# First gate/up pair by plain block products, first down operands prepared earlier, and attention paced at 0.48

## The chip, the cores and the metric

The kernel runs on one core of one Trainium2 chip. The metric is device time in microseconds (us), from the launch of the program to its end; three runs of the kernel before gave 1980.32, 1982.52 and 1985.81 us, and the median, 1982.52 us, is the number to compare with. A profiled execution of its own is used for all reading of time inside the kernel.

The engines are named as the profile names them: PE does matmuls (PEld is its weight load), DVE and ACT do elementwise work, POOL does some elementwise work and issues DMAs, SP issues DMAs only. Each engine works through its own instruction list in order.

## The reference

Two batches go through one encoder layer with shared weights: the "prompt" (512 tokens) and the "sample" (1024 tokens), 1024 wide.

```python
h = rmsnorm(x, norm_mix_w)
proj = h @ w_in                       # 1024 x 4096: HGRN2 inputs and attention q, k, v
o_hgrn = gated linear recurrence, both directions, 4 heads
o_na = neighbourhood_attention(rmsnorm(q), rmsnorm(k), v, na_rpb)   # 8 heads, 16 x 64 grid
x = x + concat([o_hgrn, o_na]) @ w_out
h2 = rmsnorm(x, norm_ffn_w)
x = x + (silu(h2 @ w_gate) * (h2 @ w_up)) @ w_down      # 1024 x 2816, twice, and 2816 x 1024
```

All of it is float32. The kernel does each large product as three matmuls: an operand is split into a rounded high part and a low part, and high x high, high x low and low x high are added in PSUM.

## The kernel before, in words

The order of the work is written out as a list of units (an input projection group, one head of the recurrence, one gate/up column block, and so on), which `drive` runs one after the other, loading the weights of the next two ahead. Beside the units runs a second stream of work: `queue` and `active` hold generators (norms, recurrence halves, the attention of a batch), and `quantum()`, which every dense unit calls after 6 matmuls, adds `mix["rate"]` to a credit; each whole credit lets `micro()` take one step of one generator. So the rate is "steps of attention per 6 dense matmuls". A scheduler then places each engine's instructions from this order, so neighbours may be exchanged.

The places that the change touches:

- **The sample's attention** (`na_jobs("s")`) runs beside the prompt's output projection and its 22 gate/up units (`gate_units_p`, `mm_tr`, L180 to L182), at a rate of 0.43. A tile step of it has the value products L604, the transposes of the probabilities L618 and the logits L636. Before the fourth-last of those units `late()` runs: `finish()` issues whatever is left of the attention, its pool is closed, and `load_oT` loads the eight head outputs of both halves of the sample (`ost<-ot_s`, L927, POOL's queue) through two staging buffers, and splits each on ACT (L928) and DVE (L929) into the tiles `os`.
- **The sample's output projection** (`out_units`, `mm_nat`, L167 to L169) multiplies `os` by `w_out`. Four PSUM banks take four token tiles; the banks come free when DVE adds the input x (L950), which SP has loaded (L937) behind the weights in its queue.
- **The sample's gate/up** (`gate_s`). The 1024 x 1024 normed input is cut in four blocks (A11, A12, A21, A22: two halves of the tokens by two halves of the width), and each pair j of 128-column gate/up blocks is made by a Strassen-Winograd scheme: seven products P1 to P7 of 12 matmuls for the gate (w = 0) and seven for up (w = 1), instead of eight plain ones each. It needs the sums S1 to S4 of input blocks and T2, T3 and two more of weight blocks. In the first pair (j = 0) the input blocks are still being made: `run()` writes out by hand when a block is filled (`fill`: ACT cast L1040, DVE remainder L1041), when the sums are formed in place (L1161 to L1170, L1207), when weight operands are made (`ahead`) and when a product begins. The first pair's weight sums run on DVE, all later ones on POOL (L1101, L1109). `taken` turns the sums of products into silu(gate) * up. From j = 1 on a plain loop does all.
- **Buffers.** Weight operands sit in the ring `w` of 5 tiles of two slots; the raw input blocks in the pool `araw`, whose memory the pool `ev1` (the results of `taken`) takes over once it is closed; the split input blocks in `x1_s`, `actR1`, `actR2` (two tiles) and `aop`.
- **The down projection** (`down_all`) is Strassen-Winograd again, 7 x 11 steps of 18 matmuls; step n needs a split gate block `ao` (from the ring `w`) and a split weight block `bo` (its own pool, opened after the gate's pools are closed). Two steps are prepared ahead.

Of the kernel before, what the change touches and what calls it, by code (L numbers as in the profile page):

```python
# [46 lines left out]
def trunk(ctx, tc, x_p, x_s, nmw, w_in, lbw, gnw, qnw, knw, rpb, w_out, nfw, w_g, w_u, w_d,  # L47
# [1001 lines left out]
    def gate_s():  # L1049
# [38 lines left out]
        def weights(wsrc, j, eng):  # L1088


            r = []
            for g in range(2):
                t = (main if g else pls["tp"]).tile([128, 1024], F32, tag="wst", bufs=2, name="wst")
                ld.dma_start(out=t.rearrange("p (k c) -> p k c", k=4),
                             in_=wsrc[g * 512:g * 512 + 512, j * 256:j * 256 + 256]
                             .rearrange("(k p) c -> p k c", p=128))
                r.append(t.rearrange("p (k n c) -> p n k c", k=4, n=2))
            B = {"11": r[0][:, 0], "12": r[0][:, 1], "21": r[1][:, 0], "22": r[1][:, 1]}

            def sub(o, x, y):  # L1100
                eng.tensor_tensor(out=o, in0=x, in1=y, op=ALU.subtract)  # L1101

            def give(n):
                if n not in ("P1", "P2", "P3") and "T2" not in B:
                    t = pls["tp"].tile([128, 2, 512], F32, tag="t", bufs=1, name="t")
                    B["T2"], B["T3"] = (t[:, i, :].rearrange("p (k c) -> p k c", k=4)
                                        for i in range(2))
                    sub(B["T3"], B["22"], B["12"])
                    eng.tensor_tensor(out=B["T2"], in0=B["T3"], in1=B["11"], op=ALU.add)  # L1109
# [13 lines left out]
        order = [(0, w, n) for n in ("P1", "P2", "P4", "P5", "P6", "P7", "P3") for w in range(2)]  # L1123
        order += [(j, w, n) for j in range(1, NP) for w in range(2)
# [3 lines left out]
        def ahead(n):  # L1128
            while len(ready) < n and todo:
                j, w, p = todo.pop(0)  # L1130
                if (j, w) not in made:
                    made[j, w] = weights((w_g, w_u)[w], j, pool if j else dve)
                ready.append(made[j, w](p))
# [6 lines left out]
        ps = {}  # L1140

        def begin(n, w, f):

            ps[n, w] = f()
            product(ps[n, w], n, ready.pop(0), False)

        def start():
            place("A11", "x1_s")
            fill("A11", raw[0, 0])
            ahead(2)  # L1150
            place("A12", "actR1")
            fill("A12", raw[0, 1])
            ahead(4)
# [19 lines left out]
        def run():  # L1173
# [3 lines left out]
            begin("P1", 0, dense_ps)  # L1177
            need(("2", "s", 6))
            fill("A22", a22, first, 2)
            begin("P1", 1, dense_ps)  # L1180
            sums(first, 2)
            begin("P2", 0, dense_ps)
# [3 lines left out]
            begin("P2", 1, dense_ps)  # L1186
            fill("A22", a22, rest, 4)
            ahead(4)
            for w in range(2):
                begin("P4", w, mix_ps)  # L1190
            sums(rest, 4)
            place("S1", "actR2")
            fill("S1", a22)
            ahead(4)
            for w in range(2):
                begin("P5", w, mix_ps)
# [3 lines left out]
            fill("S2", a11)  # L1200
            ahead(4)
# [34 lines left out]

            for w in range(2):
                s[1, w] = tmp("s1", 2)
                act.copy(out=s[1, w], in_=ps["P1", w])
                taken(w, "A11", ps["P2", w], s[1, w])  # L1240
            for w in range(2):
                begin("P6", w, dense_ps)
                s[2, w] = plus(tmp("u2", 2), ps["P6", w], s[1, w])
            ahead(4)
            for w in range(2):
                product(ps["P6", w], "P7", ready.pop(0), True)
                s[3, w] = plus(s[1, w], ps["P6", w], s[1, w])
            ahead(7)
            for w in range(2):
                taken(w, "A22", ps["P5", w], s[3, w])  # L1250
                taken(w, "A21", ps["P4", w], s[3, w])
                product(ps["P5", w], "P3", ready.pop(0), True)
                taken(w, "A12", ps["P5", w], s[2, w])
            store_g(0, 0, 512, G, ev)
            bank = {"P1": "X", "P2": "X", "P4": "W", "P6": "Y", "P7": "Y", "P5": "Z", "P3": "Z"}
            for j, w, n in order[14:]:
                ahead(7)
                x = bank[n], w
# [22 lines left out]

    def down_all():
# [16 lines left out]
        def load(n):  # L1299
            if n >= len(steps):  # L1300
                return
            i, j = steps[n]
            a = (pl if n % 2 else main).tile([128, 1024], F32, tag="wst", bufs=2,
                                             name="wst")[:, :768]
            ld.dma_start(out=a, in_=g_d[order[i][0]][j])
# [72 lines left out]
        for n in range(2):  # L1378
            prep(n)
# [28 lines left out]
    def weave(a, b_):  # L1408
        r = []
        for x, y in zip(a, b_):  # L1410
# [21 lines left out]
                    set_mix(0.43, 1))  # L1432
# [71 lines left out]
```

## Time and profile before

| | us |
|---|---|
| median of three runs | 1982.52 |
| lowest, highest run | 1980.32, 1985.81 |
| profiled execution | 1981.45 |
| span of the profiled execution (first to last instruction) | 1979.7 |
| PE busy | 1930.4 |
| DVE, ACT, POOL busy | 1259.8, 825.7, 410.3 |

The profiled execution took 1981.45 us, of which the span is 1979.7 us and 1.75 us lie around it. PE is the engine to watch: it is busy for nearly the whole span. A row of the waits says which instruction of an engine waited for which other engine's. A row of the timeline is a run of equal instructions with the start of the first, the time to the end of the last, their count, and in brackets the idle time of the engine before them with what ended it. Matmuls are pipelined, so two rows of matmuls overlap by a little; their pace is read from start to start.

### The profile page before, as it was taken

The page shows a single profiled execution, that of the slowest core. Times are in us where ns is not written, and L with a number is a line of the kernel's source. Part 1 is how long each engine was busy: PE and PEld are TensorE (multiplying, and loading weights), DVE is VectorE, ACT ScalarE, POOL GpSimd, SP SyncE. Part 2 cuts the span into 40 slices and gives each one's busy share as a digit, 9 for nine tenths or more (in the row PEclk, how much of TensorE's full clock was granted, in tenths as well). Part 3 has the DMA queues.
Part 4 walks back from the last instruction along what each step waited for, and adds up shares of the span by engine and source line. Part 5 has one row for each costly group of instructions (what it writes and reads, how often), then busy time and mean ns, then how long its engine had stood idle before and what let it go on. Part 6 is the DMA issues. An engine that isn't in the chain of part 4 may idle for free.

```text
span 1979.7 us, 31155 instructions
## 1 busy us (share of the span) xinstructions
PE 1930.4 (98%) x11890; PEld 1551.9 (78%) x11890; DVE 1259.8 (64%) x2487; ACT 825.7 (42%) x1546; POOL 410.3 (21%) x416
## 2 busy tenths in 40 slices
PE   7999999999999999999999898999999999999999
PEld 5777787778788788888887676788888887888887
DVE  7687535575765667857555349766666665675643
ACT  5555445553543545645554226322322222333331
POOL 1200000000000010212213200646445533441400
PEclk9999999999999999999999999999999999999999
DMA  7832364432122164654444621233323327663442
GB/s 238 270 100 92 113 214 125 142 106 86 44 76 91 60 222 137 194 159 151 151 126 151 242 80 44 95 112 111 96 92 104 114 78 254 198 205 122 138 155 98
DMA packets 226508, 266.61 MB, mean 135 GB/s; under 512 B 19653, under 2 KB 161115, under 8 KB 226103
## 3 DMA queue, kind: packets, MB, share of 16 engines
q1 hardware_dynamic: 188448, 186.30, 30.6%
q0 software_dynamic: 12672, 38.80, 5.5%
q10 hardware_dynamic: 25239, 39.52, 5.5%
q8 instruction: 94, 1.54, 0.3%
q14 instruction: 55, 0.45, 0.1%
HBM read 194.72 MB, written 70.20 MB: 134 GB/s over the span
## 4 chain that ended last, share of the span: by engine, by line
PE 84%; DVE 7%; DMA 5%; issue 2%; ACT 2%; POOL 0%; ACTq 0%; SPq 0%; DVEq 0%; POOLq 0%
PE pd L1046 21%; PE pm L1046 16%; PE pd L180 7%; PE pd L167 6%; PE pd L181 6%; PE pd L182 6%; PE pd L168 6%; PE pd L169 6%; PE pm L312 2%; PE pm L604 2%; PE pm L618 1%; PE pm L636 1%; DMA ost<-ot_s 1%; PE pm L451 1%; DVE w L110 1%
## 5 line engine op out<-in xcount | busy, mean ns | idle before, releaser
L110 DVE TENSOR_TENSOR w<-wst,w 128x1024 fp32r<-128x1024 f32 x128 | 160.2, 1254 | 106.5 <-ACT w L109 105.7
L1046 PE MATMUL pd<-bo,ao 128*128 128x512 f32 x792 | 199.2, 398 | 3.4 <-DVE bo L1041 3.4
L109 ACT CAST w<-wst 128x1024 fp32r<-128x1024 f32 x128 | 134.3, 1050 | 143.5 <-PE pd L182 57.9
L1046 PEld LDWEIGHTS pd<-bo,ao 128*128 128x128 f32 x792 | 149.8, 189 | 40.0 <-DVE bo L1041 3.8
L1046 PE MATMUL pm<-bo,ao 128*128 128x512 f32 x594 | 151.0, 396 | 0.0
L180 PE MATMUL pd<-h2p,w 128*128 128x512 f32 (+1 forms) x368 | 142.0, 386 | 0.1
L181 PE MATMUL pd<-h2p,w 128*128 128x512 f32 (+1 forms) x368 | 141.0, 383 | 0.0
L182 PE MATMUL pd<-h2p,w 128*128 128x512 f32 (+1 forms) x368 | 140.9, 383 | 0.0
L927 POOL DMA_DIRECT2D ost<-ot_p x8 | 4.3, 540 | 624.8 <-ACT Kn L378 610.4
L1046 PEld LDWEIGHTS pm<-bo,ao 128*128 128x128 f32 x594 | 111.7, 188 | 27.0
L1046 PE MATMUL pm<-opS,w 128*128 128x512 f32 x528 | 129.2, 394 | 2.0 <-DVE sg L1219 1.5
L167 PE MATMUL pd<-w,hs 128*128 128x512 f32 x320 | 130.7, 408 | 0.0
L1046 PE MATMUL pd<-opS,w 128*128 128x512 f32 x528 | 129.2, 394 | 1.2 <-DVE u L1219 1.2
L1046 PE MATMUL pd<-opA,w 128*128 128x512 f32 x528 | 128.9, 393 | 0.0
L169 PE MATMUL pd<-w,hs 128*128 128x512 f32 x320 | 125.6, 393 | 0.0
L168 PE MATMUL pd<-w,hs 128*128 128x512 f32 x320 | 125.5, 392 | 0.0
L1046 PEld LDWEIGHTS pm<-opS,w 128*128 128x128 f32 x528 | 99.0, 188 | 25.6 <-DVE sg L1219 1.9
L1046 PEld LDWEIGHTS pd<-opS,w 128*128 128x128 f32 x528 | 99.0, 188 | 24.8 <-DVE u L1219 2.0
L1046 PEld LDWEIGHTS pd<-opA,w 128*128 128x128 f32 x528 | 99.0, 188 | 22.1
L1040 ACT CAST w<-wst 128x512 fp32r<-128x512 f32 x110 | 64.9, 618 | 122.5 <-PE pd L1046 59.3
L1041 DVE TENSOR_TENSOR w<-wst,w 128x512 fp32r<-128x512 f32 x110 | 102.5, 949 | 15.8 <-ACT w L1040 15.4
L1041 DVE TENSOR_TENSOR bo<-B,bo 128x512 fp32r<-128x512 f32 x55 | 53.5, 974 | 85.0 <-ACT bo L1040 85.0
(245 smaller groups left out, 4308.3 us busy)
## 6 DMA issues: line engine op xcount, KB each, us to landing
wst<-in_w_in_dram SPq DMA_DIRECT2D x68, 512.0 KB, 4.0
wst<-in_w_gate_dram SPq DMA_DIRECT2D x44, 512.0 KB, 3.8
wst<-in_w_up_dram SPq DMA_DIRECT2D x44, 512.0 KB, 3.8
wst<-g_S SPq DMA_DIRECT2D x44, 384.0 KB, 3.1
wst<-g_A SPq DMA_DIRECT2D x33, 384.0 KB, 3.6
g_S<-S POOLq DMA_DIRECT2D x44, 256.0 KB, 2.7
pj_s<-ev ACTq DMA_DIRECT2D x40, 256.0 KB, 2.2
bias<-bias_d SPq DMA_DIRECT2D x192, 48.0 KB, 2.8
```

Of the source, the lines that this page charges most:

```text
L109: act.copy(out=w[:, 0, :], in_=s)
L110: dve.tensor_tensor(out=w[:, 1, :], in0=s, in1=f32(w[:, 0, :]), op=ALU.subtract)
L167: pe.matmul(ps, lhsT=xh, rhs=w[:, 0, j, :], start=k == 0, stop=False)
L168: pe.matmul(ps, lhsT=xh, rhs=w[:, 1, j, :], start=False, stop=False)
L169: pe.matmul(ps, lhsT=xl, rhs=w[:, 0, j, :], start=False, stop=k == NK - 1)
L180: pe.matmul(ps[:, ts], lhsT=wv[:, 0, k, :], rhs=xh, start=k == 0, stop=False)
L181: pe.matmul(ps[:, ts], lhsT=wv[:, 0, k, :], rhs=xl, start=False, stop=False)
L182: pe.matmul(ps[:, ts], lhsT=wv[:, 1, k, :], rhs=xh, start=False, stop=k == NK - 1)
L312: pe.matmul(ps[i:i + n, c * n:c * n + n], lhsT=lhsT[:, c * 128 + i:c * 128 + i + n], rhs=rhs(c * 128 + i), start=True, stop=True)
L1040: act.copy(out=dst[0], in_=src)
L1041: dve.tensor_tensor(out=dst[1], in0=src, in1=f32(dst[0]), op=ALU.subtract)
L1046: pe.matmul(ps, lhsT=l[a], rhs=r[b_], start=start and i == 0, stop=stop and i == 2, skip_group_check=more)
```

## The change

Three things are changed.

1. The first pair of the sample's gate/up is made by plain products: for each of gate and up the output blocks 11, 12, 21 and 22 are two input blocks times two weight blocks each (24 matmuls, eight such groups). There is no weight sum and no sum of products for this pair; A21 is split as an operand of its own; S1 moves to the pool `aop`, S4 to `actR2`, in the tile that A21 had; the eight weight blocks of the first pair take eight slots of the ring, and three operands of the second pair are made before S4 is filled.
2. `down_first` loads and splits the operands of the down projection's first two steps. It is called ahead of the second-last product of the last pair, and takes its memory from the staging buffers and the ring of the gate's weights. The loop of `down_all` begins with these.
3. The rate of the sample's attention is 0.48 steps a quantum instead of 0.43.

```diff
-        def weights(wsrc, j, eng):
+        def weights(wsrc, j):
...
             def give(n):
+                if n in B:
+                    o = slot()
+                    d = [o[:, i, :].rearrange("p (k c) -> p k c", k=4) for i in range(2)]
+                    split(d, B[n])
+                    return d
...
-        order = [(0, w, n) for n in ("P1", "P2", "P4", "P5", "P6", "P7", "P3") for w in range(2)]
-        order += [(j, w, n) for j in range(1, NP) for w in range(2)
+        order = [(j, w, n) for j in range(1, NP) for w in range(2)
                   for n in ("P1", "P6", "P2", "P7", "P5", "P4", "P3")]
...
+        def begin(c, w, f):
+
+            ps[c, w] = f()
+            for i, l in enumerate("12"):
+                o, r = A["A" + c[0] + l], first_b[w][1][l + c[1]]
+                for k in range(4):
+                    three(ps[c, w], [r[h][:, k, :] for h in range(2)], o[k],
+                          i == 0 and k == 0, i == 1 and k == 3)
...
-            begin("P1", 0, dense_ps)
+            begin("11", 0, dense_ps)
+            blocks(0, "12", "22")
             need(("2", "s", 6))
+            place("A21", "actR2")
             fill("A22", a22, first, 2)
-            begin("P1", 1, dense_ps)
-            sums(first, 2)
-            begin("P2", 0, dense_ps)
+            fill("A21", a21, first, 2)
+            begin("12", 0, dense_ps)
+            blocks(1, "11", "21")
             need(("2", "s", 7))
             close_pool("xn_s")
             open_pool("aop", "left")()
-            begin("P2", 1, dense_ps)
+            begin("11", 1, dense_ps)
             fill("A22", a22, rest, 4)
...
+            begin("12", 1, dense_ps)
+            place("S1", "aop")
+            fill("S1", a22, step=2)
             for w in range(2):
-                begin("P5", w, mix_ps)
+                begin("21", w, mix_ps)
             sums2(first, 2)
             sums2(rest, 4)
             place("S2", "actR2")
-            fill("S2", a11)
-            ahead(4)
+            fill("S2", a11, step=2)
+            for w in range(2):
+                begin("22", w, mix_ps)
             place("S3", "x1_s")
             fill("S3", a21)
-            place("S4", "aop")
...
+            ahead(3)
+            place("S4", "actR2")
             fill("S4", a12, step=2)
...
             for w in range(2):
-                taken(w, "A22", ps["P5", w], s[3, w])
...
+                for c in ("11", "12", "21", "22"):
+                    taken(w, "A" + c, ps[c, w])
...
+                if (j, w, n) == order[-2]:
+                    gate["down"] = down_first()
...
+    def down_first():
+
+        bs = main.tile([128, 2, 1024], F32R, tag="w", bufs=5, name="bs")
+        got = {}
+        for n in range(2):
+            a = main.tile([128, 1024], F32, tag="wst", bufs=2, name="wst")[:, :768]
+            ld.dma_start(out=a, in_=g_d["A11"][n])
+            b = main.tile([128, 1024], F32, tag="wst", bufs=2, name="wst")[:, :512]
+            ld.dma_start(out=b, in_=w_d[2 * n * 128:2 * n * 128 + 128, 0:512])
+            ao = main.tile([128, 2, 1024], F32R, tag="w", bufs=5, name="ao")
+            ao = [ao[:, k, :768] for k in range(2)]
+            bo = [bs[:, k, n * 512:n * 512 + 512] for k in range(2)]
+            split(bo, b)
+            split(ao, a)
+            got[n] = ao, bo
+        return got
...
-        for n in range(2):
-            prep(n)
+        ready.update(gate["down"])
...
-                    set_mix(0.43, 1))
+                    set_mix(0.48, 1))
```

Where the instructions stand is shown at three places. On PE, in the prompt's gate/up, the last attention products (L604) of the sample stand in the kernel before inside unit 19 of 0 to 21 (its gate half, `pd_11587`):

```order
L618 MATMUL pm_11426<-ident_67,pr_11408 128x128 x3
L604 MATMUL pm_11435<-pT_11430,vb_11144 64x128
L182 MATMUL pd_11523<-h2p00_8216,w_10920 128x512
L180 MATMUL pd_11587<-h2p00_8216,w_11046 128x512
L604 MATMUL pm_11435<-pT_11432,vb_11144 64x128
L604 MATMUL pm_11435<-pT_11430,vb_11144 64x128
L604 MATMUL pm_11435<-pT_11432,vb_11144 64x128
L604 MATMUL pm_11435<-pT_11430,vb_11144 64x128
L604 MATMUL pm_11435<-pT_11432,vb_11144 64x128
L181 MATMUL pd_11587<-h2p01_8217,w_11046 128x512
```

and in the changed kernel inside the up half (`pd_11300`) of unit 17, whose last 12 matmuls follow them:

```order
L181 MATMUL pd_11300<-h2p01_8230,w_10906 128x512
L182 MATMUL pd_11300<-h2p00_8229,w_10906 128x512
L604 MATMUL pm_11393<-pT_11376,vb_10999 64x128
L604 MATMUL pm_11393<-pT_11378,vb_10999 64x128
L604 MATMUL pm_11393<-pT_11376,vb_10999 64x128
L604 MATMUL pm_11393<-pT_11378,vb_10999 64x128
L604 MATMUL pm_11393<-pT_11376,vb_10999 64x128
L604 MATMUL pm_11393<-pT_11378,vb_10999 64x128
L180 MATMUL pd_11300<-h2p00_8229,w_10906 128x512
L181 MATMUL pd_11300<-h2p01_8230,w_10906 128x512
```

Up to the first matmul of the sample's output projection 143 dense matmuls follow the last L604 in the kernel before, and 204 in the changed one.

On ACT, where the first gate/up pair passes into the second, the changed kernel has (`w_12928` is the ring tile with P6 and P2 of the second pair's up half, `th` the tanh that frees the first PSUM bank, `opS4` the sum S4):

```order
L1040 CAST w_12879<-wst_12815 128x512
L1040 CAST w_12885<-wst_12815 128x512
L1040 CAST w_12885<-wst_12903 128x512
L1040 CAST opS4_12829<-a01_12156 128x1024 x2
L1040 CAST w_12928<-t_12924 128x512
L1040 CAST w_12928<-wst_12905 128x512
L1248 ACTIVATE th_12839<-pd_12520 128x512
L1248 ACTIVATE th_12843<-pd_12571 128x512
```

In the kernel before S4 is filled ahead of the first results of the pair (L1239, L1229), and the results stand between the casts of the weights of the second pair. In the changed one all eight results of the first pair come after S4 and after the two casts into `w_12928`; that tile is the one that held blocks 12 and 22 of the first pair's up weights.

On ACT at the end of the gate/up, the kernel before splits `ao` of step 0 early but `bo` only behind the last stores of the gate:

```order
L1040 CAST ao_15798<-wst_15786 128x768
L1229 ACTIVATE th_15578<-sg_15576 128x512
L1229 ACTIVATE th_15599<-sg_15597 128x512
L1265 COPY s1_15617<-pd_15604 128x512
L1035 DMA g_A11_102<-G_15646 128x512
L1035 DMA g_A22_104<-G_15674 128x512
L1040 CAST bo_15799<-B11_0_15735 128x512
L1040 CAST ao_15804<-wst_15789 128x768
```

and the changed kernel has both steps (`bs` is the tile that holds their two weight blocks) ahead of those stores:

```order
L1040 CAST bs_15655<-wst_15658 128x512
L1248 ACTIVATE th_15556<-sg_15554 128x512
L1248 ACTIVATE th_15577<-sg_15575 128x512
L1271 COPY s1_15595<-pd_15582 128x512
L1040 CAST ao_15660<-wst_15656 128x768
L1040 CAST bs_15655<-wst_15667 128x512
L1040 CAST ao_15669<-wst_15665 128x768
L1035 DMA g_A11_102<-G_15624 128x512
```

So the four casts of the first two steps moved ahead of the last two result stores, and the first `bo` that still waits for the gate's memory is that of the third step.

## Rows read from the trace of the kernel before

**Rows 1.** The page, part 1: busy us, share of the span, instructions.
```profile
PE 1930.4 (98%) x11890; PEld 1551.9 (78%) x11890; DVE 1259.8 (64%) x2487; ACT 825.7 (42%) x1546; POOL 410.3 (21%) x416
```

**Rows 2.** Waits of PE: waiting instruction, releaser, us in total, times, longest.
```profile
PE pd L167 <- DVE x L950: 8.3, 1, 8.3
PE pm L1046 <- ACT w L1040: 7.2, 1, 7.2
PE pd L1046 <- DVE bo L1041: 3.4, 1, 3.4
...
PE pm L618 <- DVE pr L675: 0.5, 1, 0.5
```

**Rows 3.** Windows, busy us: PE, PEld, DVE, ACT, POOL; then clock, DMA share, GB/s.
```profile
1120.00:1132.00 12.00, 3.73 (x10) 2.83 (x10) 4.24 (x7) 1.96 (x4) 2.71 (x5) 0.72 0.80 302
...
1224.00:1232.00 8.00, 5.79 (x16) 4.19 (x17) 8.00 (x14) 4.26 (x9) 0.00 (x0) 0.59 0.20 66
...
1650.00:1655.00 5.00, 5.00 (x16) 3.92 (x16) 5.00 (x6) 0.00 (x0) 3.51 (x5) 0.66 1.00 254
```

**Rows 4.** Timeline of PE in the sample's output projection, around the pause.
```profile
1128.48 0.76 PE L167 MATMUL pd<-w,os 128*128 128x512 f32 x1 [8.27 <-DVE x L950]
...
1131.84 0.40 PE L169 MATMUL pd<-w,os 128*128 128x512 f32 x1
```

**Rows 5.** Timeline of PE in the steady gate/up loop: start, us, count.
```profile
1296.59 2.88 PE L1046 MATMUL pd<-opA,w 128*128 128x512 f32 x12
...
1316.00 2.88 PE L1046 MATMUL pd<-opA,w 128*128 128x512 f32 x12
```

**Rows 6.** Timelines of PE, POOL, ACT and SP between attention and output projection.
```profile
1064.29 0.87 PE L604 MATMUL pm<-pT,vb 128*64 128x128 f32 x10
...
1120.76 0.54 POOL L927 DMA_DIRECT2D ost<-ot_s  x1 [5.91 <-DMA x<-in_x_sample_dram]
...
1126.39 0.62 ACT L928 CAST os<-ost 128x512 fp32r<-128x512 f32 x1 [4.26 <-DMA ost<-ot_s]
...
1110.47 3.48 SPq L937 DMA_DIRECT2D x<-in_x_sample_dram  x6
```

**Rows 7.** Timeline of PE in the first gate/up pair.
```profile
1202.73 3.24 PE L1046 MATMUL pd<-opA,w 128*128 128x512 f32 x13
...
1212.42 1.03 PE L141 MATMUL pm<-ident,xn 128*128 128x128 f32 x8
1213.21 3.04 PE L1046 MATMUL pd<-opA,w 128*128 128x512 f32 x12
...
1226.21 5.21 PE L1046 MATMUL pm<-opA,w 128*128 128x512 f32 x12 [7.15 <-ACT w L1040]
...
1257.98 2.20 PE L1046 MATMUL pd<-opA,w 128*128 128x512 f32 x9
```

**Rows 8.** Timelines of ACT, DVE and POOL in that pair: prices of single operations.
```profile
1239.92 0.62 ACT L1040 CAST w<-t 128x512 fp32r<-128x512 f32 x1 [0.79 <-POOL t L1101]
...
1251.32 0.63 ACT L1229 ACTIVATE th<-sg 128x512 f32<-128x512 f32 x1 [5.67 <-DVE sg L1219]
...
1226.03 1.28 DVE L1041 TENSOR_TENSOR w<-wst,w 128x512 fp32r<-128x512 f32 x2
...
1246.67 3.23 DVE L1041 TENSOR_TENSOR w<-wst,w 128x512 fp32r<-128x512 f32 x2
...
1253.79 0.68 DVE L1230 SCALAR_TENSOR_TENSOR sg<-th,sg 128x512 f32<-128x512 f32 x1
...
1247.73 1.62 POOL L1109 TENSOR_TENSOR t<-t,wst 128x512 f32<-128x512 f32 x1
```

**Rows 9.** Timeline of PE at the start of the down projection.
```profile
1646.02 0.40 PE L1046 MATMUL pd<-bo,ao 128*128 128x512 f32 x1
1649.79 4.37 PE L1046 MATMUL pd<-bo,ao 128*128 128x512 f32 x11 [3.36 <-DVE bo L1041]
...
1655.38 2.96 PE L1046 MATMUL pd<-bo,ao 128*128 128x512 f32 x12
```

More of the change, by code (lines that the diff above doesn't have):

```diff
@@ L1100, in sub @@
             def sub(o, x, y):
-                eng.tensor_tensor(out=o, in0=x, in1=y, op=ALU.subtract)
+                pool.tensor_tensor(out=o, in0=x, in1=y, op=ALU.subtract)
             def give(n):
+                if n in B:
[3 more added lines that the diff above has]
+                    return d
                 if n not in ("P1", "P2", "P3") and "T2" not in B:
@@ L1108, in give @@
                     sub(B["T3"], B["22"], B["12"])
-                    eng.tensor_tensor(out=B["T2"], in0=B["T3"], in1=B["11"], op=ALU.add)
+                    pool.tensor_tensor(out=B["T2"], in0=B["T3"], in1=B["11"], op=ALU.add)
                     sub(B["12"], B["12"], B["11"])
@@ L1131, in ahead @@
                 if (j, w) not in made:
-                    made[j, w] = weights((w_g, w_u)[w], j, pool if j else dve)
+                    made[j, w] = weights((w_g, w_u)[w], j)
                 ready.append(made[j, w](p))
@@ L1138, in product, with blocks @@
                       k == 3, more)
[L1140 to L1145, printed above, removed]
+        ps, first_b = {}, {}
+        def blocks(w, *names):
+            if w not in first_b:
+                first_b[w] = weights((w_g, w_u)[w], 0), {}
+            give, got = first_b[w]
+            for n in names:
+                got[n] = give(n)
+        def begin(c, w, f):
[5 more added lines that the diff above has]
+                          i == 0 and k == 0, i == 1 and k == 3)
         def start():
@@ L1149, in start @@
             fill("A11", raw[0, 0])
-            ahead(2)
+            blocks(0, "11")
             place("A12", "actR1")
             fill("A12", raw[0, 1])
-            ahead(4)
+            blocks(0, "21")
             place("A22", "actR1")
@@ L1185, in run @@
             open_pool("aop", "left")()
-            begin("P2", 1, dense_ps)
+            begin("11", 1, dense_ps)
             fill("A22", a22, rest, 4)
-            ahead(4)
-            for w in range(2):
[L1190 to L1195, printed above, removed]
-                begin("P5", w, mix_ps)
+            fill("A21", a21, rest, 4)
+            blocks(1, "12", "22")
+            sums(first, 2)
+            sums(rest, 4)
+            begin("12", 1, dense_ps)
+            place("S1", "aop")
+            fill("S1", a22, step=2)
+            for w in range(2):
+                begin("21", w, mix_ps)
             sums2(first, 2)
@@ L1237, in run @@
             for w in range(2):
[L1238 to L1249, printed above, removed]
-                taken(w, "A22", ps["P5", w], s[3, w])
-                taken(w, "A21", ps["P4", w], s[3, w])
-                product(ps["P5", w], "P3", ready.pop(0), True)
-                taken(w, "A12", ps["P5", w], s[2, w])
+                for c in ("11", "12", "21", "22"):
+                    taken(w, "A" + c, ps[c, w])
             store_g(0, 0, 512, G, ev)
             bank = {"P1": "X", "P2": "X", "P4": "W", "P6": "Y", "P7": "Y", "P5": "Z", "P3": "Z"}
-            for j, w, n in order[14:]:
+            for j, w, n in order:
                 ahead(7)
+                if (j, w, n) == order[-2]:
+                    gate["down"] = down_first()
                 x = bank[n], w
@@ L1302, in load @@
             i, j = steps[n]
-            a = (pl if n % 2 else main).tile([128, 1024], F32, tag="wst", bufs=2,
-                                             name="wst")[:, :768]
-            ld.dma_start(out=a, in_=g_d[order[i][0]][j])
+            a = None
+            if n >= 2:
+                a = (pl if n % 2 else main).tile([128, 1024], F32, tag="wst", bufs=2,
+                                                 name="wst")[:, :768]
+                ld.dma_start(out=a, in_=g_d[order[i][0]][j])
             bs = {}
```

1 line of the change is left out of this document (removed).

## The prediction

> **What bounds the kernel now.** I read the page's busy times first, then the waits of PE, then the timeline of PE around each long wait. The reader is to see that PE is busy 98% of the span [rows 1], so there are only two ways to gain: fewer matmuls, or the few places where PE stands still. The change adds matmuls, so all its gain must come from pauses. The waits of PE name three long ones [rows 2]: 8.3 us in the sample's output projection (L167, for DVE's addition of x), 7.2 us in the first gate/up pair (L1046, for an ACT cast) and 3.4 us at the start of the down projection (L1046, for a weight remainder on DVE). The windows show that each costs more than its length: behind each the granted clock of the stretch is 0.72, 0.59 and 0.66 [rows 3], so part of it ran at the lower of the two levels, 1.2 instead of 2.4 GHz. The undisturbed pace is read where the loop runs steadily: 84 matmuls from 1296.59 to 1316.00, so 19.41 / 84 = 0.231 us for one [rows 5].
>
> **Attention at 0.48.** No matmul is added or removed here; the attention's steps move ahead. In the order 143 dense matmuls stand behind its last product before, 204 after: it ends 61 x 0.231 = 14.1 us earlier against the dense work. What hangs on its end: it ends at 1064.29 + 0.87 = 1065.2; then its sixteen output tiles are loaded through two staging buffers and split, the last load issued at 1120.76, the last cast at 1126.39 [rows 6]. DVE's addition of x stands in DVE's list behind the last split, so PE got its PSUM bank only at 1128.48, after 8.27 us [rows 4]. The next eight matmuls took 1131.84 - 1128.48 = 3.36 us in place of 8 x 0.231 = 1.85, another 1.5 us. With the whole chain 14.1 us earlier the last cast falls at about 1112.3, and PE would have stopped at 1128.48 - 8.27 = 1120.2: 7.9 us to spare. So all of 8.27 + 1.5 = **9.8 us** go. What is late next: the x loads. Six of them were issued at 1110.47 [rows 6], and POOL's last load waited until 1120.76 for one to land, so they took about ten us together. SP's list now has a gate weight load ahead of the first x load, and that load takes a staging buffer of the attention outputs, so it waits for the second-last split. With that split 14 us earlier it still lets x go before 1110; I take no cost, with 0 and 9.8 us as the bounds.
>
> The denser attention could make PE wait for the softmax. At the old distances PE waited 0.5 us once for the probabilities [rows 2]; in the new order the last six tile steps stand 12 dense matmuls (2.8 us) apart, the others 24 or more. I take nothing; the upper bound is the slow rival below.
>
> **The first pair.** Before, PE goes from the first product at 1202.73 to the second pair's second matmul at 1257.98, so 55.0 us to its first [rows 7]. Its content is 168 matmuls, 38.8 us, and two groups of transposes of 1213.21 - 1212.42 = 0.8 us each, together 40.4. So 14.6 us are lost: the 7.15 us wait at 1226.21, its slow matmuls, and small waits behind. DVE was busy for 8.00 of 8 us of the stretch from 1224 to 1232 [rows 3]: this pair was bound by DVE.
>
> After, the content is 8 x 24 = 192 matmuls, 44.4 us, so 24 x 0.231 = 5.5 us are added, plus 1.6 of transposes: 46.0. DVE's load falls: eight weight sums on DVE and twelve sums of products go, two weight remainders and the split of A21 come. What PE needs in time is A21 and A22. They are due behind 96 matmuls and both groups of transposes, 23.8 us after the start; the last token tile's transposes stand behind 48 matmuls, 12.7 us after the start. That leaves 11 us for two copies, two casts and two remainders of about 0.6 us each [rows 8], about 4 us in a chain. Seven us are to spare, so I count no wait there.
>
> A new wait stands at the pair's end. The first result (tanh on ACT, then DVE's product), which frees the PSUM bank for the second pair's P1, stands in ACT's list behind two casts into the ring tile `w_12928`. That tile is the one with the last group's weights, blocks 12 and 22 of up, so ACT waits there until the very last matmul of the pair; the results queue behind it, and PE waits for them. The price by [rows 8]: two casts of 0.62, tanh 0.63, DVE 0.68, together 2.55, and some 0.15 for three hand-overs: 2.7 us of pause. S4's split, in the tile of A21, is no later: A21 is read last 12 matmuls before the end. What the clock makes of this pause the trace does not show at that length. The bounds are nothing, and what the 3.36 us pause cost at the down start: 17 matmuls from 1649.79 to 1655.38, 5.59 us in place of 3.93, so 1.7 [rows 9]. The nearest pause shown is that one, so I take 1.7. The pair gains 55.0 - 46.0 - 2.7 - 1.7 = **4.6 us**; the bounds are 9.0 (no pause) and 0.
>
> POOL speaks against this part. The second pair's weight sums on POOL now begin as soon as their weights have landed, beside DVE's work on A21 and A22. Two remainders took 1.28 us alone at 1226.03 and 3.23 at 1246.67, with a POOL sum of 1.62 at 1247.73 inside that stretch [rows 8]: DVE lost 1.95 us. Four sums at that price hold DVE up for 4 x 1.62 = 6.5 us at most, inside the 7 us to spare, so the sum is unchanged; if they are not, 1 to 3 us come back as a wait for A21. The Trainium skill ("SBUF — State Buffer", Who interferes with whom) says that a VectorE instruction with two SBUF inputs and a GpSimd one that reads SBUF hold each other up completely, the one that started first keeping the ports. The row agrees: the loss is about the POOL instruction's own time. By that rule the price is the whole 6.5 us, and the gain of this part stays the same or falls by what exceeds the cover.
>
> **The start of the down projection.** Before, the first matmul at 1646.02 was alone, the next came at 1649.79 after 3.36 us idle, and the second step began at 1655.38 [rows 9]: 9.36 us for 18 matmuls that are worth 4.16. The wait was for `bo`, whose memory the gate held. Now both steps' operands lie in the gate's own buffers. The added work (two loads of each kind on SP, four casts, four remainders of 0.6 to 1 us) is no new work, only the same moved ahead, into a stretch in which ACT and DVE wait for PE. On SP the first weight load waits for the staging buffer of the last weights and holds back the later `g` and weight loads; on ACT the first cast of `bs` waits for it, with two tanh and the copy of P1 behind it. These loads were issued in the same place before, for `ao`. The third step's `bo` is due two steps, 8.3 us, after the gate's end: covered. So 9.36 - 4.16 = **5.2 us**; the bounds are 5.2 and 0 (the stall moves to the third step).
>
> **Sum.** 9.8 + 4.6 + 5.2 = 19.6 us. The profiled execution took 1981.45, which gives 1961.9; the median of the runs is 1.07 us higher, which gives **1963 us**.
>
> **Rivals.**
> - *The output projection keeps a pause.* x now queues behind a load that needs the attention's staging buffer. For: ten us for six loads, and the weights, x and attention outputs all land in the same stretch, DMA share 0.80 [rows 3]. Against: the buffer comes free 14 us earlier. If all is lost, 1973; if half, 1968.
> - *The first pair gives nothing.* DVE and POOL hold each other up, A21 comes late, or the new wait at the pair's end is longer. For: the 3.23 us row, and a pair that was DVE-bound. Against: fewer DVE instructions, seven us to spare. 1968.
> - *The down stall only moves* to the third step's `bo`. For: its memory is still the gate's. Against: 8.3 us of cover. 1968.
> - *Slower than before: the attention becomes the bound.* At 0.48 its 32 tile steps stand closer, and PE waits for each softmax. The gain of 19.6 us is gone at 0.6 us a step, and from 25.6 / 32 = 0.8 us a step on the kernel is measurably slower, at 1988.5 or more. For: the last six steps stand 2.8 us apart. Against: one wait of 0.5 us in all at the old rate.
> - *Two of the first three together*: 1973 to 1978, or the rate moves nothing that counts.
>
> **How the numbers follow.** My forecast, about 1963, has 58 in 100; without the clock's cost and the new pause it would be 1958.6, the foot of its own range. The output projection's rival has 14, the first pair's 12, the down start's 6, two together 6, slower 4. About 0.3%, 6 us, is what a measurement of this kernel can tell from no change, so faster means below 1976.6 and slower above 1988.5. The first four cases are faster: 90. The pairs of failures count as the same: 6; slower 4. The range, 1957 to 1973, takes in the first four cases and leaves out what is at most 2 in 10.
>
> **What would show it.** Right: PE has no wait on L950 in the sample's output projection, and the granted clock is 1.00 there; from the first product to the second pair 50 to 52 us in place of 55.0, with one pause of 2.5 to 3 us at the end, its releaser the first result on DVE; 18 matmuls of the first down step in about 4.2 us. Wrong: waits of PE on L618 beyond 1 us in all, a wait for A21 or A22 inside the first pair, a wait of PE at the third down step, or x landing after its bank is due.

## The result and the profile after

The changed kernel takes 1965.06 us (median of five runs, 1963.75 to 1971.47), the kernel before 1981.82 beside it: a ratio of 0.9924 over all runs, 95% interval 0.9905 to 0.9944, so 15 us less (11 to 19); the medians differ by 16.8. The forecast was 1963, range 1957 to 1973. The profiled execution is the slowest of its five, 1971.47 us, and its span is 10.3 us below the span before. By stages, from markers that both timelines of PE have: up to the prompt's first gate product it is 4.2 us *late* (770.29 before, 774.50 now), in a part that the change does not touch; a second profile of the same kernel stands at 769.85 there, so this is no effect of the change. The stages behind that marker are compared below.

First the page's busy times and the waits of PE in the changed kernel (waiting instruction, releaser, us in total, times, longest). They answer to [rows 1, 2].

```profile
PE 1932.4 (98%) x11914; PEld 1555.3 (79%) x11914; DVE 1248.0 (63%) x2460; ACT 822.4 (42%) x1537; POOL 407.0 (21%) x416
```

```profile
PE pm L539 <- DVE dd L531: 4.2, 3, 1.8
PE pd L1046 <- DVE sg L1249: 2.7, 1, 2.7
...
PE pd L167 <- DVE G L1011: 2.3, 1, 2.3
...
PE pm L618 <- DVE pr L675: 0.8, 1, 0.8
```

There are 24 matmuls more, as the change says. All three long waits of [rows 2] are gone. Two are new: 2.7 us for the first pair's first result, which was forecast, and 2.3 us in the sample's output projection, which was not: PE waits there no longer for x (L950) but for `G` of L1011, the tanh product of a *prompt* gate unit. The timeline of PE there, then DVE's, ACT's and POOL's; they answer to [rows 4, 6].

```profile
1106.27 0.39 PE L169 MATMUL pd<-w,os 128*128 128x512 f32 x1
1108.99 0.79 PE L167 MATMUL pd<-w,os 128*128 128x512 f32 x1 [2.34 <-DVE G L1011]
...
1112.42 0.40 PE L169 MATMUL pd<-w,os 128*128 128x512 f32 x1
```

```profile
1107.02 1.32 DVE L929 TENSOR_TENSOR os<-ost,os 128x512 fp32r<-128x512 f32 x2 [2.22 <-ACT os L928]
1108.26 0.68 DVE L1011 SCALAR_TENSOR_TENSOR G<-th,pd 128x512 f32<-128x512 f32 x1
```

```profile
1106.37 1.25 ACT L928 CAST os<-ost 128x512 fp32r<-128x512 f32 x2 [2.82 <-DMA ost<-ot_s]
...
1107.52 0.59 ACT L1010 ACTIVATE th<-pd 128x512 f32<-128x512 f32 x1
1114.08 0.62 ACT L928 CAST os<-ost 128x512 fp32r<-128x512 f32 x1 [5.96 <-DMA ost<-ot_s]
```

```profile
1054.03 0.54 POOL L927 DMA_DIRECT2D ost<-ot_s  x1 [21.88 <-PE pm L618]
1061.15 0.74 POOL L1030 TENSOR_TENSOR S<-G 128x256 f32<-128x256 f32 x1 [6.58 <-DVE G L1013]
...
1066.81 1.07 POOL L927 DMA_DIRECT2D ost<-ot_s  x2
```

The chain reads from the bottom. With the attention earlier, the splits of its outputs stand earlier in the lists of ACT and DVE too: before, 10 of the 16 stood ahead of the last prompt unit's `G`, now 15. So `G`, which frees PE's bank for the third token tile, waits for two more loads to land (1106.37 on ACT); the unit's tanh, which `G` reads, stands behind the same two casts (1107.52). And the chain of loads did not start as early as its first row: POOL's list has a gate pair's sums between the first load (1054.03) and the second (1066.81). The last cast still came at 1114.08 (1126.39 before; 1112.3 was forecast); counted from the marker, which stands 4.2 us later here, that is 16.5 us earlier, where 14.1 was forecast. So x was in time. PE lost from the end of twelve matmuls to 1112.42 about 4.0 us: 2.34 of waiting, the rest in matmuls 0.43 us apart in place of 0.233.

The first pair, on PE (answers to [rows 7]), then the ACT list that PE waited for at its end (answers to [rows 8]):

```profile
1202.90 5.82 PE L1046 MATMUL pd<-opA,w 128*128 128x512 f32 x24
...
1226.97 22.56 PE L1046 MATMUL pm<-opA,w 128*128 128x512 f32 x96
1252.22 4.58 PE L1046 MATMUL pd<-opA,w 128*128 128x512 f32 x12 [2.69 <-DVE sg L1249]
1256.63 2.95 PE L1046 MATMUL pd<-opS,w 128*128 128x512 f32 x12
```

```profile
1246.81 2.00 ACT L1040 CAST opS<-a 128x1024 fp32r<-128x1024 f32 x2 [1.70 <-issue]
1249.62 0.62 ACT L1040 CAST w<-t 128x512 fp32r<-128x512 f32 x1 [0.81 <-PE pm L1046]
1250.15 0.61 ACT L1040 CAST w<-wst 128x512 fp32r<-128x512 f32 x1
1250.67 0.59 ACT L1248 ACTIVATE th<-pd 128x512 f32<-128x512 f32 x1
```

192 matmuls and two groups of transposes took 46.6 us (46.0 forecast), the pause 2.69 (2.7), and the twelve matmuls behind it 1256.63 - 1252.22 = 4.41 where 2.8 is their pace: 1.6 (1.7). From the first product to the second pair's first matmul it took 1252.22 - 1202.90 = 49.3 us; the sign named was 50 to 52. The two casts into the ring tile start only when PE lets go, and tanh stands behind them, as the order said.

The start of the down projection (answers to [rows 9]), and the windows that answer to [rows 3] (busy us of PE, PEld, DVE, ACT, POOL; clock, DMA share, GB/s):

```profile
1642.14 2.91 PE L1046 MATMUL pd<-bs,ao 128*128 128x512 f32 x12
1644.89 1.52 PE L1046 MATMUL pm<-bs,ao 128*128 128x512 f32 x6
1646.25 2.88 PE L1046 MATMUL pd<-bs,ao 128*128 128x512 f32 x12
...
1650.33 2.96 PE L1046 MATMUL pd<-bo,ao 128*128 128x512 f32 x12
```

```profile
1106.00:1116.00 10.00, 7.66 (x27) 5.78 (x26) 3.63 (x6) 3.30 (x5) 4.75 (x8) 0.83 0.94 271
1252.00:1257.00 5.00, 4.78 (x14) 3.85 (x15) 3.48 (x6) 1.36 (x3) 1.54 (x2) 0.66 0.28 105
1642.00:1651.00 9.00, 9.00 (x41) 7.42 (x40) 5.49 (x7) 3.67 (x6) 5.39 (x7) 1.00 1.01 366
```

The 18 matmuls of the first step took 4.1 us, there is no wait at the third step, and the granted clock is 1.00: that part went as forecast.

### The profile page after: what moved, and what is told of

The parts are those of the page before. It is cut to its first block, busy times and chain, and to the rows that moved or that the text cites. A ratio compares the mean times of both kernels' runs of the same rounds, so it can differ in the third digit from the quotient of the medians.

```text
span 1969.4 us, 31179 instructions
## 1 busy us (share of the span) xinstructions
PE 1932.4 (98%) x11914; PEld 1555.3 (79%) x11914; DVE 1248.0 (63%) x2460; ACT 822.4 (42%) x1537; POOL 407.0 (21%) x416
## 4 chain that ended last, share of the span: by engine, by line
PE 51%; issue 1%; DMA 1%; POOL 1%; DVE 0%; ACT 0%; POOLq 0%; DVEq 0%
PE pd L1046 22%; PE pm L1046 16%; PE pd L180 2%; PE pd L181 2%; PE pd L182 2%; PE pd L167 2%; PE pd L169 1%; PE pd L168 1%; DMA ost<-ot_s 1%; PE pm L618 1%; PE pm L604 1%; PE pm L636 1%; PE pm L141 0%; PE pm L539 0%; POOL S L1032 0%
## 5 line engine op out<-in xcount | busy, mean ns | idle before, releaser
L1046 PE MATMUL pd<-bo,ao 128*128 128x512 f32 x768 | 191.3, 396 | 0.0
L1046 PEld LDWEIGHTS pd<-bo,ao 128*128 128x128 f32 x768 | 144.3, 188 | 34.9
L1046 PE MATMUL pd<-opA,w 128*128 128x512 f32 x576 | 142.0, 397 | 2.7 <-DVE sg L1249 2.7
L1046 PEld LDWEIGHTS pd<-opA,w 128*128 128x128 f32 x576 | 109.0, 190 | 28.4 <-DVE sg L1249 3.1
L1041 DVE TENSOR_TENSOR w<-wst,w 128x512 fp32r<-128x512 f32 x108 | 107.6, 1013 | 19.7 <-ACT w L1040 19.3
L1046 PE MATMUL pd<-opS,w 128*128 128x512 f32 x480 | 117.4, 393 | 0.0
L1046 PE MATMUL pm<-opS,w 128*128 128x512 f32 x480 | 116.9, 392 | 0.0
L1046 PEld LDWEIGHTS pd<-opS,w 128*128 128x128 f32 x480 | 90.2, 188 | 20.8
L1046 PEld LDWEIGHTS pm<-opS,w 128*128 128x128 f32 x480 | 90.2, 188 | 20.3
```

The costliest lines, as they stand in the source:

```text
L1041: dve.tensor_tensor(out=dst[1], in0=src, in1=f32(dst[0]), op=ALU.subtract)
L1046: pe.matmul(ps, lhsT=l[a], rhs=r[b_], start=start and i == 0, stop=stop and i == 2, skip_group_check=more)
```

## Experiments

Each time stands beside runs of the kernel before on the same chip, whose medians were 1981.05, 1980.71 and 1979.67 us in the three sets; ratios are to them, over all runs, with 95% intervals. The stage times below come from one profile of each. Two stages recur: the *attention stretch* (first gate product of the prompt to the first matmul of the sample's output projection) and the *output projection* (from there to the first product of the first pair). Before: 327.4 and 105.1 us. Changed, first profile: 329.2 and 99.2.

### One part at a time

Three kernels, each the kernel before with one part of the change. The rate:

```
-                    set_mix(0.43, 1))
+                    set_mix(0.48, 1))
```

> The kernel before with the attention's rate of 0.48 alone. Theory: the wait for x's addition goes (8.27 + 1.5 us), but the last prompt gate unit's result now stands in DVE's list behind 15 splits of attention outputs instead of 10, so the third token tile of the sample's output projection waits about 2.3 us for its bank, and with the slow matmuls behind it some 4 us come back: a gain of 5.9 us, about 1976 where before has 1981.8. Rival 1, the prediction's term as it stands: 9.8 us, 1972. Rival 2: the denser attention itself costs PE time, so the stretch from the prompt's gate to the sample's output projection grows by 2 us or more: a gain of 4 us or less, 1978 or more.

Measured: 1975.06 us, ratio 0.9965 (0.9952 to 0.9977), 6.9 us less. The wait came as the theory said, at the same place:

```profile
1103.39 0.50 PE L167 MATMUL pd<-w,os 128*128 128x512 f32 x1 [2.65 <-DVE G L1011]
```

but no slow matmul stands behind it this time, and the output projection took 98.1 us: 7.0 less than before, between theory and rival 1. The attention stretch grew by 1.2 us, so a small piece of rival 2 is there too.

The first pair alone is the changed kernel with these lines back as they were, and without the helper of the down operands:

```
-                    set_mix(0.48, 1))
+                    set_mix(0.43, 1))
...
-                if (j, w, n) == order[-2]:
-                    gate["down"] = down_first()
```

> The plain first pair alone: attention at 0.43 and the down projection's start as before. Theory: the 7.15 us wait goes, 24 matmuls and one pause of 2.7 us with slow matmuls behind it come: a gain of 4.0 us (the prediction's term was 4.6), about 1978. Rival 1: the pair gives nothing by itself, 1982, and what the changed kernel's trace shows there comes from the earlier x of the new rate. Rival 2: POOL's weight sums hold DVE up while A21 is made, seen as a wait of PE inside the pair ahead of its last product.

Measured: 1975.4 us, ratio 0.9963 (0.9949 to 0.9978), 7.3 us less. From the first product to the second pair's second group of matmuls it took 53.8 us where 57.8 stood before: 4.0, the theory's size, and the new pause at its end is the only long wait:

```profile
1251.14 4.61 PE L1046 MATMUL pd<-opA,w 128*128 128x512 f32 x12 [2.69 <-DVE sg L1249]
1255.59 2.97 PE L1046 MATMUL pd<-opS,w 128*128 128x512 f32 x12
```

The 4.0 lies just below the interval of the whole time (4.4 to 10.1; the medians differ by 5.7). In this profile the span is 5.7 us shorter than before, and the 1.7 that are not the pair's come in pieces of 0.5 us or less from stages that the edit does not touch, so the rest is not shown to be the pair's. The wait for x stood in its output projection at 5.83 us instead of 8.27 with nothing changed there: this wait, too, differs from run to run.

The down operands alone: the kernel before with the helper and these lines (the loop's own loads of the first two steps go).

```
+                if (j, w, n) == order[-2]:
+                    gate["down"] = down_first()
...
+        ready.update(gate["down"])
```

> The first two down operands made ahead, alone: rate and first pair as before. Theory: the 3.36 us wait goes with its slow matmuls, 18 matmuls of the first down step in 4.2 us: a gain of 5.2 to 5.4 us, about 1976.5. Rival: the loads moved ahead delay the last gate pair or the third down step, and less than 3 us are left.

Measured: 1974.41 us, ratio 0.9969 (0.9957 to 0.9981), 6.1 us less (3.8 to 8.5). From the first down step to the third it took 8.2 us, before 13.6: 5.4, as expected.

The three add up to 20.3 us, the whole change gives 15.1 and in a second set 16.2 (by the medians 18.3 against 16.8 and 18.1). With intervals of 2 to 4 us to either side of each that is no contradiction, so an interaction is neither shown nor excluded.

### The changed kernel once more

> The changed kernel once more, unchanged. Theory: the wait for the last prompt gate unit's result in the sample's output projection depends on when two loads of attention outputs land, which differs between runs, so this profile shows it with another length, anywhere from 0 to 3 us (2.34 in the first profile), and with or without slow matmuls behind it; the median is 1964 to 1968. Rival: it is a fixed price of the new order and stands again at 2.3 us with the same slow matmuls, about 4 us together.

Measured: 1962.66 us, ratio 0.9918 (0.9904 to 0.9931); the profiled execution's span was 1959.5. The theory holds for the wait; its median, 1964 to 1968, was missed by 1.3 us. The two loads landed so that the last `G` began 2.3 us after the projection's first matmul (4.6 in the first profile), and PE, which needs its bank after 2.8, had next to no wait in the output projection: 95.5 us in place of 99.2.

```profile
1101.32 0.68 DVE L1011 SCALAR_TENSOR_TENSOR G<-th,pd 128x512 f32<-128x512 f32 x1
```

And the pause at the pair's end stood there with the same length, but cost nothing more:

```profile
1243.83 3.06 PE L1046 MATMUL pd<-opA,w 128*128 128x512 f32 x12 [2.69 <-DVE sg L1249]
1246.73 2.96 PE L1046 MATMUL pd<-opS,w 128*128 128x512 f32 x12
```

Twelve matmuls in 2.90 us, where the same twelve took 4.41 in the first profile. The granted clock of these 5 us (1243 to 1248) is 1.00, where it was 0.66 in the first profile (1252 to 1257). So the same pause of the same kernel is followed by matmuls at the lower clock in one run and not in another.

### The pause at the pair's end

```
-            for w in range(2):
-                begin("22", w, mix_ps)
+            for i in range(2):
+                for w in range(2):
+                    begin("22", w, mix_ps, (i,))
...
```

The last argument picks one half of a product: 0 reads A21, 1 reads A22.

> The changed kernel, with the last two products of the first pair interleaved by halves: both halves that read A21 first, then both that read A22. A21's memory, where S4 goes, is then free 24 matmuls before the pair's end instead of 12, and the two first tanh stand ahead of the casts into the ring tile that waits for the last matmul. No work is added or removed. Theory (the pause at the pair's end is the ACT list's order): the 2.7 us wait falls below 1 us, and the 1.6 us of slow matmuls behind it go too: 3 to 4.3 us faster than the changed kernel, about 1961.5. Rival 1: the first result waits for S4's own split on DVE, which only moves by 2.8 us at most, or for the remainders ahead of it: a pause of 1.5 us stays, 1 to 2 us faster. Rival 2: the clock falls behind any pause: only the wait's own 2 us are won, and slow matmuls are still there.

Measured: 1959.28 us, ratio 0.9888 (0.9873 to 0.9904); once more in the third set:

> The changed kernel with the halves alone, once more beside the others. Theory (the wait for the last prompt gate unit depends on when loads land): between 0 and 3 us of it stand in this profile, and the median lies 1 to 2 us above the version with SP's queue, 1958 to 1960. Rival: its first median, 1959.28, came from lucky runs, and it is no faster than the changed kernel, 1963 to 1965.

Measured: 1958.47 us, ratio 0.9890 (0.9875 to 0.9905). The pause is gone, not halved, and the twelve matmuls behind it run at full pace (2.86 and 2.84 us), so rivals 1 and 2 fall. The last group of the pair and the next product of PE in the first of the two profiles, and the ACT list there:

```profile
1220.03 22.56 PE L1046 MATMUL pm<-opA,w 128*128 128x512 f32 x96
1242.43 3.03 PE L1046 MATMUL pd<-opA,w 128*128 128x512 f32 x12
```

```profile
1240.88 0.59 ACT L1250 ACTIVATE th<-pd 128x512 f32<-128x512 f32 x1
1242.40 0.60 ACT L1250 ACTIVATE th<-pd 128x512 f32<-128x512 f32 x1 [0.94 <-DVE sg L1251]
1242.90 0.61 ACT L1040 CAST w<-t 128x512 fp32r<-128x512 f32 x1
```

The first two tanh now stand ahead of the cast `w<-t`, which stood in front of them and waited for the pair's last matmul (1249.62 in the changed kernel).

The pair took 49.3 us to the second group, 8.4 less than before: near the 9.0 that the prediction gave as its upper bound. Two sets agree at 0.989, so it was no luck. Against the changed kernel's 0.9918 that is some 6 us, more than the 3 to 4.3 expected. One profile of each can't say where the rest comes from. In the second profile the wait for `G` stood at 2.24 us, with slow matmuls behind it, 0.43 us apart (99.2 us for the output projection); in the first at 0.54 (95.9 us).

```profile
1102.20 0.50 PE L167 MATMUL pd<-w,os 128*128 128x512 f32 x1 [2.24 <-DVE G L1011]
...
1105.23 0.63 PE L169 MATMUL pd<-w,os 128*128 128x512 f32 x1
```

### The chain of attention outputs

```
-                st.dma_start(out=s, in_=dram[b, "o", k][:, u * 512:u * 512 + 512])
+                (ld if b == "s" else st).dma_start(out=s, in_=dram[b, "o", k][:, u * 512:u * 512 + 512])
```

> The changed kernel, with the sample's attention outputs loaded on SP's queue in place of POOL's, where the gate results' sums and stores stand between them. Theory A (POOL's list holds the loads up: the second was issued 12.8 us after the first): the chain ends some 10 us sooner, the wait for the last prompt gate unit is gone, 2 to 4 us faster than the changed kernel. Theory B (the chain is paced by two staging buffers, some 5 us for each two loads): it ends hardly sooner and the wait stays, no change within 2 us. Rival C: the loads wait in SP's list for their buffers and hold up the gate weights behind them; PE waits for a weight cast (L109) and the kernel is slower than the changed one.

Measured: 1961.87 us, ratio 0.9906 (0.9892 to 0.9919). Theory A is right about the chain: the first two loads were issued within 2.8 us, the last casts began at 1096.52 (1106.25 in the changed kernel's profile of the same set), there was no wait in the output projection, which took 95.2 us, and the weights behind the loads came in time.

```profile
1096.52 1.33 ACT L928 CAST os<-ost 128x512 fp32r<-128x512 f32 x2 [1.29 <-DMA ost<-ot_s]
```

The 2 to 4 us against the changed kernel are not shown: the medians differ by 0.8 and the intervals overlap. The four runs lie within 1.1 us (1961.33 to 1962.38), the five of the changed kernel beside them within 5.9.

Two outputs in each buffer, on POOL's queue as before:

```
-            for k in range(8):
+            for k in range(0, 8, 2):
...
-                s = pls[pl].tile([128, 1024], F32, tag=tag, bufs=bufs, name="ost")[:, :512]
+                s = pls[pl].tile([128, 2, 512], F32, tag=tag, bufs=bufs, name="ost")
...
```

The edit is written out here for the sample alone; the prompt's outputs keep one to a buffer.

> The changed kernel, with two attention outputs in each staging buffer (the second half of each lay unused), cast and split together: eight rounds of the chain in place of sixteen. Theory B (the two buffers pace the chain): the last split comes 10 us or more sooner, no wait for the last prompt gate unit, the sample's output projection runs without a pause at full clock: 2 to 4 us faster than the changed kernel, 1962 or so. Theory A (POOL's list): the end moves by 5 us or less, and a wait may stay. If the wait costs nothing on the median run, the time stays the same within 1 us.

Measured: 1965.36 us, ratio 0.9925 (0.9911 to 0.9939). Theory B is right about the chain: its last split ended at 1097.5. It is wrong about the wait, which stayed and was longer, 3.14 us, for the same `G`. Its cause is another one, on ACT:

```profile
1104.40 1.04 ACT L109 CAST w<-wst 128x1024 fp32r<-128x1024 f32 x1 [5.80 <-DMA wst<-in_w_out_dram]
1104.45 0.34 ACTq L949 DMA_DIRECT2D wrow<-in_norm_ffn_w_dram  x1
1105.35 0.59 ACT L1013 ACTIVATE th<-pd 128x512 f32<-128x512 f32 x1
```

```profile
1092.24 0.37 SPq L1097 DMA_DIRECT2D wst<-in_w_gate_dram  x1
1097.54 0.37 SPq L1097 DMA_DIRECT2D wst<-in_w_up_dram  x1
1098.63 8.46 SPq L108 DMA_DIRECT2D wst<-in_w_out_dram  x3
```

The other order of the lists put two weight loads of the first pair (`gate`, 1092.24, and `up`, 1097.54), which need a staging buffer of the attention outputs, ahead of three of the output projection's own weights on SP. The cast of those was late on ACT, and the unit's tanh stood behind it. So one wait took the place of another. Here the slow matmuls behind the pause cost more than elsewhere: thirteen took 5.70 us in place of 3.03, 2.7 us.

Both edits together:

> The changed kernel with both: the last two products of the first pair by halves, and two attention outputs in each staging buffer. No work is added. Theory: neither pause is left, so it beats the changed kernel by 5 to 8 us: 1957 to 1960. Rival: the runs with halves alone had no pause in the output projection anyway, and this one is no faster than they were, 1959.

Measured, with both edits: 1962.16 us, ratio 0.9909 (0.9895 to 0.9922). The theory falls. The rival is right that this is no faster than the halves alone, but it looked for 1959 and no pause: the same wait stood at 2.60 us with slow matmuls behind it (99.4 us for the output projection), and part of what the halves won was lost there.

The halves with SP's queue, and the halves with the rate at 0.52:

> The changed kernel with both edits that went with a better median: the first pair's last two products by halves, and the sample's attention outputs loaded on SP's queue. Theory: neither the 2.7 us pause at the pair's end nor a pause in the sample's output projection is left, in any run, and no slow matmuls behind them: 4 us less than with SP's queue alone, ratio to before 0.988, about 1957.5. Rival: on SP's queue the weights behind the loads come late when the attention outputs do, and what the halves win is lost there: 1960 or more.

Measured: 1957.39 us, ratio 0.9882 (0.9867 to 0.9897). This is the theory's 1957.5: neither pause is left in its profile, and the output projection takes 95.2 us. It is faster than the kernel before and than the changed one, which stands at 0.9918 (0.9904 to 0.9931): the intervals do not touch. Against SP's queue alone (0.9892 to 0.9919) they overlap by a little.

> The halves, with the attention's rate at 0.52 in place of 0.48, which puts its last product 73 dense matmuls, 16.9 us, further ahead of the sample's output projection; the last prompt gate unit's result then stands behind all sixteen splits, which have 16.9 us more. Theory: no pause is left in the output projection, as on SP's queue: about 1957.5. Rival (the prediction's slow rival): the tile steps stand closer and PE waits for the softmax (L618), 1.2 us in all at 0.48, more than 4 us at 0.52: 1961 or more.

Measured: 1958.1 us, ratio 0.9888 (0.9872 to 0.9905). There is no long wait in the output projection (95.2 us), no wait on L618 among those of 0.4 us and more, and the attention stretch takes 326.7 us. The slow rival does not begin at 0.52. Halves alone, with SP and with 0.52 are not told apart by their intervals.

## Why the prediction was right, point by point

- **Pace, content and clean parts.** The pair's content (46.0 forecast, 46.6 measured), its pause (2.7, 2.69) and the down start (5.2, 5.4 by the steps) hold. Of the down start's gain about 1.5 us are slow matmuls of the kernel before, which the profile with the rate alone did not have: with it as the measure, 3.9.
- **Output projection: 9.8 us.** The term is right for a projection without a pause: 105.1 before, 95.2 in the three kernels that had none, 9.9 less. The step that failed is "so all of 8.27 + 1.5 = 9.8 us go". It counted the last cast against x and did not ask what else moves behind the splits: the last prompt unit's `G` stands behind five more of them. In the first profile that left 5.9 of the 9.8, in the second 9.6. The sign named for this term, a granted clock of 1.00 there, did not come in the first profile (0.83 from 1106 to 1116). The rival "keeps a pause" came partly true by another mechanism than the one named: x and the gate weight load were in time.
- **The first pair: 4.6 us.** To the second pair's second group it gained 4.0 in the first profile and 5.5 in the second (57.75 before, 52.22 after): the clock's 1.7 is paid in some runs and not in others. The cover for A21 was 5.0 us where 7 were worked out: its last remainder ended at 1221.97, its first product began at 1226.97.
- **DVE against POOL.** The feared 6.5 us did not arise: only three of POOL's sums ran early (1206.34 to 1210.98), the next at 1235.65. Beside the three, DVE operations took 1.26, 1.23 and 1.12 us that take 0.22, 0.15 and 0.68 elsewhere in the same list: 2.6 us lost, inside the cover. Whether these are the 2 us that the cover lacked is not shown. Where they met again, at 1239, two remainders took 3.22 us, alone 1.29, in a part that PE does not wait for. The Trainium skill's rule ("SBUF — State Buffer", Who interferes with whom) is borne out in the loss of 1.9 us beside sums of 1.3 and 1.8, and by the row as by the rule nothing of it reaches the sum.
- **The attention at 0.48** was taken at nothing. The attention stretch is 1.0 to 1.8 us longer in all nine profiles at 0.48 (1.8 in both of the changed kernel). A wait of 1.1 to 1.9 us at L539, for `dd` in eight of them, now falls into it, and 0.6 to 1.5 us on L618 where 0.5 stood. So one sign of being wrong, more than 1 us on L618, came in the second profile (1.3) without the slow rival behind it. At 0.52 the stretch is not longer, so it is not the density as such; which order of list entries makes it was not tried.
- **The sum.** 1963 for a median of 1965.06 and 1962.66. By stages the three terms gave 5.9 + 4.0 + 5.4 = 15.3 us in the first profile and 9.6 + 5.5 + 5.4 = 20.5 in the second, less 1.8 for the attention stretch, where 19.6 was forecast. So the terms' mechanisms hold, but that the median falls within 2 us is in part luck: it hangs on how many runs have the wait for `G`, which the sum did not have, and the slow matmuls, which it took as a fixed price. The difference between profiles of one kernel (spans of 1969.4 and 1959.5) is as large as a term.

## What to carry to other kernels

When work is moved earlier, look in the lists of the engines that do it for what now stands *behind* it, not only at what was waiting for it: an evacuation of a PSUM bank behind a cast that waits for a DMA was here a pause of PE of 0 to 2.7 us, depending on when the loads landed. The pause at the seam of the two pairs was the order of one list; freeing the buffer one half product earlier took it away without any work less. And when one wait is taken away, look at what takes its place: loading twice as much per buffer ended the chain 10 to 18 us earlier (against the two profiles of the changed kernel) and only gave the place at the seam to the next late load.

## What the runs showed of the hardware

A pause of PE had no fixed price in clock. After the same wait of 2.69 us, the next twelve matmuls took 4.41 us in one profile of the changed kernel and 2.90 in the other, 4.45 with the pair alone and 4.45 with SP's queue. In the output projection, waits of 2.24, 2.34, 2.60 and 3.14 us for `G` had a slow stretch behind them, and one of 2.65, with the rate alone, had none (granted clock 1.00 from 1103 to 1108). And after the wait at the down start the eleven matmuls that took 4.37 us in the kernel before took, with the rate alone:

```profile
1642.94 2.83 PE L1046 MATMUL pd<-bo,ao 128*128 128x512 f32 x11 [3.37 <-DVE bo L1041]
```

At these three places the profiles show thirteen pauses of 2.2 to 3.4 us: behind three nothing was lost, behind nine 1.3 to 1.6 us, and behind one (3.14 us) 2.7. The length of the pause does not tell which. The granted clock of whole executions (0.992 to 1.000) goes with their times: the changed kernel's ten runs go from 1961.59 at 0.999 to 1971.47 at 0.996. The Trainium skill ("TensorE: Matmul & The Clock Gate", Part 1: The HAM clock gate) says that the gate's timing is not tied to the kernel's start, so that the slow matmuls at a start differ from run to run of the same kernel. The two profiles of the changed kernel (4.41 and 2.90 us) agree, for a pause in the middle. A term of this kind is better put as a chance than as a middle value.
